# Holding back expert loads until the first gather, splitting expert 0's weights earlier, clearing row tiles earlier

## The chip, the cores and the metric

The kernel runs on one core of a Trainium2 chip. The metric is the device time of one execution in microseconds (us). The core's engines are named as the profile names them: PE (TensorE, matmul), DVE (VectorE), ACT (ScalarE), POOL (GpSimd) and SP (SyncE, which here only issues transfers). Each engine runs its own list of instructions in order. Transfers between the chip's memory and the core's are done by 16 DMA engines; an instruction on SP or POOL only starts them.

## The reference

The program is one decoder block: a forgetting attention and an S5 state-space mixer in parallel, whose result is projected by `w_out` and added to the input, and then a mixture of experts. The change touches the last product, the routing and the experts:

```
g_prob = softmax(xt @ w_rg + b_rg);  g_top, g_sel = top_k(g_prob, 1)      # 1 of 4 groups
e_prob = softmax(logits of the 8 experts of that group)
e_top, e_idx = top_k(e_prob, 2);  w = g_top * e_top / sum(e_top)
for e in range(32):
    h = silu(xt @ w_gate[e]) * (xt @ w_up[e])         # (1024, 256)
    y = y + combine[:, e:e+1] * (h @ w_down[e])       # (1024, 1024)
```

There are 1024 tokens of 1024 numbers. An expert's weights are `w_gate` and `w_up` (1024 x 256 each) and `w_down` (256 x 1024), together 3 MB in float32. All 32 experts' weights, 96 MB, are read once.

## The kernel before

The last third of the program has two stages.

**Routing.** The product with `w_out` runs in 16 units (`units`), half a row block of 128 tokens each. Behind each unit come the pieces of `tail(i)`: residual, norm, router, softmax, the choice of two experts and the place of each token in its expert's list. They leave the normed rows `xn_d` in the chip's memory (the last block's two halves are stored by SP, L1276 and L1275) and, at the very end, the table `ix`: for each expert the row numbers of up to 96 tokens (L1311, DVE).

**Experts.** For each of 32 experts POOL gathers its rows by an indirect transfer (`gather_rows`, L1328, issued two experts ahead) into one of three tiles `XG`; PE transposes them (`turn_rows`, L1339), ACT copies the transposed rows as `xh` (L1342) and DVE makes the remainder `xl` (L1343), which in all gives each operand as a high and a low part. Then `gate_up` (24 matmuls, L1352 to L1354), `hidden` (silu on ACT, product `hh` on DVE, transposition, copy `hT` on ACT, L1368), `down` (8 matmuls, L1377) and a scatter that adds the rows into the output (L1379, POOL).

**Weights.** `load_expert` issues six transfers of 512 KB for an expert on SP: four tiles `raw_e` (gate and up, each in two halves, L1083) and two tiles `wd` (down, L1087). There are five sets of these tiles, so loads run up to five experts ahead; a load waits until its tile is free, and all those behind it on SP wait with it. `split_expert` turns an expert's `raw_e` tiles into a high part `weh` by 8 casts on ACT (L1101) and a low part `wel` by 8 subtractions on DVE (L1102), 4 of each for either half; the first half is `raw_e` 0 and 1, which the first matmuls of `gate_up` use.

**What sets the order.** The program is written in Python, and a scheduler orders each engine's instructions by priorities in which program order counts; `after(...)` puts the instructions of its block behind a given one, and `keep_in_program_order` keeps the loads on SP in the order in which they are written. The table `AHEAD` says in front of which unit how many loads of which expert are written: `8: [(2, 6)]` means six of expert 2 ahead of unit 8. Expert o's remaining loads follow in the expert loop by calls `load(o, n)`.

Before, `AHEAD` puts all loads of experts 0 to 3 and four of expert 4 among the units, and expert 4's two `wd` loads behind the last unit. The tiles `XG` are cleared by POOL (`rows_tile`, L1321): two behind the routing, the third behind the second gather. Expert 0's weights are split behind `ix`, and expert 1's first half behind that.

Of the kernel before, what the change touches and what calls it, by code (L numbers as in the profile page):

```python
# [10 lines left out]
F32 = mybir.dt.float32  # L11
# [5 lines left out]
ALU = mybir.AluOpType  # L17
AX = mybir.AxisListType

P = 128  # L20
D = 1024
S = 1024
# [11 lines left out]
NE = 32  # L34
# [8 lines left out]
def hybrid_block(ctx: ExitStack, tc: tile.TileContext, t, out):  # L43

    nc = tc.nc

    def pool(stack, name, bufs=1, side=None, space=None):
        kw = {}
        if side:
            kw["side"] = side  # L50
        if space is not None:
            kw["space"] = space
        return stack.enter_context(tc.tile_pool(name=name, bufs=bufs, **kw))
# [6 lines left out]
    def mmtile():  # L60
        return psA.tile([P, 512], F32, tag="A", name="psA_t")

    def smtile():
        return psB.tile([P, 512], F32, tag="B", name="psB_t")

    def f32(ap):
        return ap.bitcast(F32)
# [4 lines left out]
    def slot(name, shape=(S,), dt=F32, where=None):  # L72
        pl, n = where or (slab, SLOTS)
        return pl.tile([P] + list(shape), dt, tag="s4", name=name, bufs=n)
# [12 lines left out]
    sp = pool(ssm_stack, "ssm_c", 1, side="right")  # L87
# [398 lines left out]
    with ExitStack() as st:  # L486
# [19 lines left out]
        for b in range(G // GB):  # L506
# [84 lines left out]
            for q4 in range(GB // 4):  # L591
# [7 lines left out]
                for r in range(4):  # L599
                    g = q4 * 4 + r  # L600
                    o = ps[:, r * P:(r + 1) * P]
# [376 lines left out]
    SR = (slabR, SLOTSR)  # L978
# [85 lines left out]
    for a in range(2):  # L1064
        nc.gpsimd.iota(ent[:, :, a, 0:1], pattern=[[P, NT], [0, 1]], base=0, channel_multiplier=1,
                       allow_small_or_imprecise_dtypes=True)
    xn_d = tc.dram_tile([S, D], F32, name="xn_d")
    tbl_d = tc.dram_tile([NE * CAP * NBLK, 2], F32, name="tbl_d")


    def load_expert(e, raws, wd):


        if isinstance(e, int):
            sel = lambda ap: ap[e]
        else:
            sel = lambda ap: ap[bass.ds(e, 1)].rearrange("o a b -> (o a) b")
        wd3 = sel(t["w_expert_down"]).rearrange("(p j) f -> p j f", j=2)
        for q in range(4):
            nm = ("w_expert_gate", "w_expert_up")[q % 2]  # L1080
            src = sel(t[nm]).rearrange("(p k) f -> p k f", k=KD)[:, q // 2 * 4:q // 2 * 4 + 4, :]
            raws[q] = raws[q]()
            tc.keep_in_program_order(nc.sync.dma_start(raws[q], src))  # L1083
            yield raws, wd
        for j in range(2):
            wd[j] = wd[j]()
            tc.keep_in_program_order(nc.sync.dma_start(wd[j], wd3[:, j, :]))  # L1087
            yield raws, wd

    def split_expert(raws, c):  # L1090

        ws = []
        for k2 in range(4):
            v = (2 * c + k2 // 2) % 3, k2 % 2
            if v not in ws_t:
                ws_t[v] = slot("weh", (2, 512), F32R), slot("wel", (2, 512), F32R)
            wh, wl = ws_t[v]
            for q in range(2):
                src = raws[k2 // 2 * 2 + q][:, k2 % 2 * 2:k2 % 2 * 2 + 2, :]
                d_ = (slice(None), slice(None), slice(q * 256, q * 256 + 256))  # L1100
                nc.scalar.copy(wh[d_], src)  # L1101
                nc.vector.tensor_tensor(wl[d_], src, f32(wh[d_]), ALU.subtract)  # L1102
            ws.append((wh, wl))
            if k2 == 1:
                yield
        yield ws
# [3 lines left out]
    def place_of(nm, shape, tiles, c, where):  # L1110
        def get():
            if c not in tiles:
# [8 lines left out]
    ahead = [load_expert(ORDER[o], [place_of("raw_e", (4, 256), raw_t, (SET[o], q), RAW[SET[o]][q]) for q in range(4)],  # L1121
                         [place_of("wd", (S,), wd_t, (o % 5, j), WD[o % 5][j]) for j in range(2)]) for o in range(NE)]
    got = []
    AHEAD = {0: [(0, 6)], 2: [(1, 6)], 8: [(2, 6)], 12: [(3, 6), (4, 2)], 14: [(4, 2)]}

    ix = rp.tile([CAP, NE], I32, name="ix")
    wts = rp.tile([CAP, NE], F32, name="wts")
    empty = rp.tile([P, NE], F32, name="empty")
    cnt = rp.tile([P, NE], F32, name="cnt")
    ptab = mmtile()  # L1130
    with ExitStack() as st:
        xp = pool(st, "x1p", 1, side="right")
# [16 lines left out]
        def product(i, n):  # L1149
            if i not in x1s:  # L1150
                x1s[i] = slot("x1", where=(SR, S2)[i - NT + 2]) if i >= NT - 2 else xp.tile([P, D], F32, name="x1", bufs=2)
                nc.gpsimd.dma_start(x1s[i], t["x"][i * P:(i + 1) * P, :])
            x1 = x1s[i]
            ns = slice(n * 512, n * 512 + 512)
            ps = mmtile()
            for k in range(KD):
                if k == KD // 2:
                    yield
                mh, ml = [v[k // 4, i // 2][:, k % 4, i % 2 * P:i % 2 * P + P] for v in (mxh, mxl)]
                wh, wl = [v[:, k % 2, :] for v in wos[n, k // 2]]  # L1160
                nc.tensor.matmul(ps, mh, wh, start=(k == 0), stop=False)
                nc.tensor.matmul(ps, mh, wl, start=False, stop=False)
                nc.tensor.matmul(ps, ml, wh, start=False, stop=(k == KD - 1))
            nc.vector.tensor_tensor(x1[:, ns], ps, x1[:, ns], ALU.add)
# [113 lines left out]
        ends = {}  # L1278
# [12 lines left out]
        for u, (i, n) in enumerate(units):  # L1291
            for o, m in AHEAD.get(u, ()):
                for _ in range(m):
                    r_ = next(ahead[o])
                got[o:] = [r_]
            pr = product(i, n)
            next(pr)
            if u == 1:
                out_splits(3)
            behind_products(u)  # L1300
            for _ in pr:
                pass
        behind_products(len(units))
        behind_products(len(units) + 1)
        for _ in range(2):
            r_ = next(ahead[4])

        pc = smtile()
        nc.tensor.matmul(pc[:, 0:NE], oneb, run, start=True, stop=True)
# [1 line left out]
        last_dve = nc.vector.tensor_tensor(ix, ptab[0:CAP, 0:NE], empty[0:CAP], ALU.add)  # L1311
# [2 lines left out]


    em_ = pool(ctx, "moe", 1, side="right")
    XG = []

    def rows_tile(where):
        XG.append(where.tile([P, S], F32, name="XG") if where is em_ else slot("XG", where=where))  # L1320
        nc.gpsimd.memset(XG[-1], 0.0)  # L1321

    rows_tile(SR)
    rows_tile(SR)
    mt = pool(ctx, "moet", 2, side="right")

    def gather_rows(xg, ix):
# [4 lines left out]
    def turn_rows(xg):  # L1332

        xh = mt.tile([P, KD, CAP], F32R, name="xh")
        xl = mt.tile([P, KD, CAP], F32R, name="xl")
        for kk in range(2):
            ps = smtile()
            for r in range(4):
                pe = nc.tensor.transpose(ps[:, r * CAP:(r + 1) * CAP], xg[0:CAP, kk * 4 + r::8], ident[0:CAP, 0:CAP])  # L1339
            dst = (slice(None), slice(kk * 4, kk * 4 + 4))  # L1340
            pv = ps[:, 0:4 * CAP].rearrange("p (a b) -> p a b", a=4)
            nc.scalar.copy(xh[dst], pv)  # L1342
            nc.vector.tensor_tensor(xl[dst], pv, f32(xh[dst]), ALU.subtract)  # L1343
        return (xh, xl), pe

    def gate_up(x, ws):
        xh, xl = x
# [40 lines left out]
    def icol(o):  # L1388
        return ix[:, ORDER[o]:ORDER[o] + 1]


    def after(*instructions):

        st = ExitStack()
        for ins in instructions:
            st.enter_context(tc.issue_after(ins.ins))
        return st

    for o in range(2):
        last_gather = gather_rows(XG[o], icol(o))  # L1400
    with tc.issue_after(last_gather.ins):
        rows_tile(em_)
    w_now = got[0]
    got.append(r_)
    got.extend([None] * (NE - 5))

    def load(o, n):
        if o < NE:
            for _ in range(n):
                got[o] = next(ahead[o])  # L1410
    with after(ends["act"], last_dve):
        *_, ws = split_expert(got[0][0], 0)
    load(5, 4)
    x, _ = turn_rows(XG[0])
    sp = split_expert(got[1][0], 1)
    next(sp)
    load(6, 2)
    behind, act, dve = None, ends["act"], last_dve
    scs = []
    for o in range(NE):  # L1420
        if o + 2 < NE:
            gather_rows(XG[(o + 2) % 3], icol(o + 2))
        ps, pe = gate_up(x, ws)
        if o + 1 < NE:
            w_next = got[o + 1]
            if o:
                with after(act, dve):
                    sp = split_expert(w_next[0], o + 1)
                    next(sp)
                load(o + 6, 2)  # L1430
        h = hidden(ps)
        dve = next(h)
        if o + 1 < NE:
            with after(pe):
                x, pe = turn_rows(XG[(o + 1) % 3])
        if behind:
            with after(pe):
                _, sc, pe = down(*behind, apart=scs[-3:])
            scs.append(sc)
            load(o + 4, 2)  # L1440
        with after(pe):
            hT, act = next(h)
        e = ORDER[o]
        behind = (hT, w_now[1], icol(o), wts[:, e:e + 1])
        if o + 1 < NE:
            with after(act, dve):
                ws = next(sp)
            load(o + 6, 2)
        w_now = w_next
# [66 lines left out]
```

## Time and profile before

| | |
|---|---|
| median of 3 runs | 1205.27 us (1204.71 to 1208.66) |
| the profiled execution | 1208.14 us, span of its instructions 1206.4 us |
| mean granted TensorE clock | 0.97 of full speed |
| PE busy | 1116.5 us, 93% of the span |
| DVE, ACT, POOL busy | 793.5, 619.5, 432.1 us |
| all transfers | 193.78 MB, of which 96 MB (in units of 1024 x 1024) are expert weights |

A share of the span is an average over many stages. In a row of the timeline, "x8" after the shapes says that eight instructions in a row were put together, the number in front of the engine is their length from first start to last end, and the bracket gives the idle time of the engine before them and what ended it. The profile's times count from the span's start; the routing ends and the expert loop begins at about 850 us.

### The profile page before, as it was taken

What the parts mean: (1) busy time and instruction counts of PE and PEld (TensorE: products, weight loads), DVE (VectorE), ACT (ScalarE), POOL (GpSimd) and SP (SyncE); (2) the same over time, 40 slices, a digit from 0 to 9 for tenths busy, and PEclk for the clock granted to TensorE, in tenths of its full rate; (3) what the DMA queues carried; (4) which work ended last, traced back from release to release, by engine and by line L of the source; (5) the groups of instructions that cost most, each with busy time, mean ns of one, the idle gap of its engine ahead of it and who ended that gap; (6) DMA issues with size and microseconds to landing.
All of it is one profiled execution on the core that took longest, in us unless ns stands there. A gap on an engine that the chain in (4) does not pass through costs nothing. (4 is left out here: it accounts for less than half of the span.)

```text
span 1206.4 us, 15940 instructions
## 1 busy us (share of the span) xinstructions
PE 1116.5 (93%) x5323; PEld 854.3 (71%) x5324; DVE 793.5 (66%) x1561; ACT 619.5 (51%) x1195; POOL 432.1 (36%) x431
## 2 busy tenths in 40 slices
PE   5899899899999999999899988998499999999995
PEld 4678778687898778888677777886366666666562
DVE  4657577667025889898987696538566666666661
ACT  5423332332335576766769553103366666666662
POOL 3025445432514474656714362103322222222211
PEclk9899899999999999999989999999699999999998
DMA  8516435330253012000622539564599999999992
GB/s 234 82 41 157 92 75 104 80 91 28 87 121 53 2 27 47 11 23 28 210 70 101 175 124 346 189 220 179 185 306 341 333 312 317 312 310 320 310 332 51
DMA packets 100919, 193.78 MB, mean 161 GB/s; under 512 B 26177, under 2 KB 55169, under 8 KB 100833
## 3 DMA queue, kind: packets, MB, share of 16 engines
q1 hardware_dynamic: 82176, 150.16, 40.8%
q0 software_dynamic: 14048, 34.17, 10.5%
q10 hardware_dynamic: 4608, 8.39, 1.9%
q8 instruction: 43, 0.70, 0.2%
q14 instruction: 44, 0.35, 0.1%
HBM read 164.30 MB, written 35.52 MB: 166 GB/s over the span
## 5 line engine op out<-in xcount | busy, mean ns | idle before, releaser
L1102 DVE TENSOR_TENSOR wel<-raw_e,weh 128x512 fp32r<-128x512 f32 x256 | 157.4, 684 | 118.8 <-ACT weh L1101 107.5
L1101 ACT CAST weh<-raw_e 128x512 fp32r<-128x512 f32 x256 | 137.0, 621 | 3.0 <-DMA raw_e<-in_w_expert_up 1.8
L910 POOL TENSOR_TENSOR sm<-sm,pe 128x256 f32<-128x256 f32 (+2 forms) x80 | 96.4, 1205 | 72.5 <-ACT pe L907 64.2
L1377 PE MATMUL psA_t<-wd,hT 128*96 128x512 f32 x256 | 117.4, 600 | 3.1 <-DMA wd<-in_w_expert_down 2.3
L1352 PE MATMUL psA_t<-weh,xh 128*96 128x512 f32 x256 | 103.7, 405 | 0.2
L1353 PE MATMUL psA_t<-wel,xh 128*96 128x512 f32 x256 | 102.0, 399 | 0.0
L183 PE MATMUL psA_t<-hTh,wgl 128*128 128x512 f32 x256 | 101.9, 398 | 0.0
L182 PE MATMUL psA_t<-hTh,wgh 128*128 128x512 f32 x256 | 101.4, 396 | 0.0
L1354 PE MATMUL psA_t<-weh,xl 128*96 128x512 f32 x256 | 101.2, 395 | 0.0
L184 PE MATMUL psA_t<-hTl,wgh 128*128 128x512 f32 x256 | 100.8, 394 | 0.0
L1379 POOL DMA_INDIRECT out_rows<-R,ix x32 | 46.1, 1441 | 128.5 <-ACT hT L1368 117.2
L793 PE MATMUL psA_t<-wqh,hTh 128*128 128x384 f32 x256 | 88.3, 345 | 0.0
L794 PE MATMUL psA_t<-wql,hTh 128*128 128x384 f32 x256 | 86.8, 339 | 0.0
L795 PE MATMUL psA_t<-wqh,hTl 128*128 128x384 f32 x256 | 86.8, 339 | 0.0
L1328 POOL DMA_INDIRECT XG<-xn_d,ix x32 | 36.5, 1140 | 139.7 <-PE psB_t L1339 132.3
L1378 ACT ACTIVATE R<-psA_t,wts 96x512 f32<-96x512 f32 x64 | 43.7, 682 | 77.1 <-PE psA_t L1377 75.0
L1377 PEld LDWEIGHTS psA_t<-wd,hT 128*96 128x96 f32 x256 | 40.4, 168 | 56.4 <-issue 49.0
L905 ACT ACTIVATE pH<-psB_t 128x512 fp32r<-128x512 f32 (+1 forms) x96 | 49.1, 512 | 38.9 <-PE psB_t L902 38.7
L908 DVE TENSOR_TENSOR pL<-pe,pH 128x256 fp32r<-128x256 f32 (+2 forms) x80 | 62.9, 798 | 6.8 <-ACT pe L907 5.9
L855 DVE TENSOR_REDUCE mx<-psB_t 128x1 f32<-128x512 f32 (+2 forms) x96 | 51.2, 550 | 7.9 <-PE psB_t L850 4.2
L183 PEld LDWEIGHTS psA_t<-hTh,wgl 128*128 128x128 f32 x256 | 48.7, 190 | 9.5 <-POOL wgl L172 0.2
L184 PEld LDWEIGHTS psA_t<-hTl,wgh 128*128 128x128 f32 x256 | 48.5, 189 | 9.5
(427 smaller groups left out, 2878.2 us busy)
## 6 DMA issues: line engine op xcount, KB each, us to landing
raw_e<-in_w_expert_gate SPq DMA_DIRECT2D x64, 512.0 KB
raw_e<-in_w_expert_up SPq DMA_DIRECT2D x64, 512.0 KB
wd<-in_w_expert_down SPq DMA_DIRECT2D x64, 512.0 KB
gate_d<-ge ACTq DMA_DIRECT2D x32, 256.0 KB
gt<-gate_d SPq DMA_DIRECT2D x16, 512.0 KB
raw_g<-in_w_in SPq DMA_DIRECT2D x12, 512.0 KB
raw_q<-in_w_in SPq DMA_DIRECT2D x48, 128.0 KB
x<-in_x SPq DMA_DIRECT2D x8, 512.0 KB
```

The costliest lines, as they stand in the source:

```text
L182: nc.tensor.matmul(ps, wh, hTh[k][:, ns], start=(k == 0), stop=False)
L183: nc.tensor.matmul(ps, wl, hTh[k][:, ns], start=False, stop=False)
L184: nc.tensor.matmul(ps, wh, hTl[k][:, ns], start=False, stop=(k == KD - 1))
L793: nc.tensor.matmul(ps[:, :384], ah, wh, start=(k == 0), stop=False)
L794: nc.tensor.matmul(ps[:, :384], ah, wl, start=False, stop=False)
L910: nc.gpsimd.tensor_tensor(sm[:, o0:], sm[:, o0:], pe[:, :n], ALU.add)
L1101: nc.scalar.copy(wh[d_], src)
L1102: nc.vector.tensor_tensor(wl[d_], src, f32(wh[d_]), ALU.subtract)
L1352: nc.tensor.matmul(ps, xh[:, k, :], wh[:, k % 2, :], start=(k == 0), stop=False)
L1353: nc.tensor.matmul(ps, xh[:, k, :], wl[:, k % 2, :], start=False, stop=False)
L1354: last = nc.tensor.matmul(ps, xl[:, k, :], wh[:, k % 2, :], start=False, stop=(k == KD - 1))
L1377: pe = nc.tensor.matmul(po, hT[:, j, :], wd[j][:, ns], start=(j == 0), stop=(j == 1))
```

## The change

1. `AHEAD` keeps only the loads of experts 0 and 1 and the four `raw_e` of expert 2. The 14 others of experts 2 to 4 (two `wd` of expert 2, six each of experts 3 and 4) are written behind the first two gathers and behind a new small transfer `first_d` on SP, which reads a few numbers of `XG[0]` and so cannot start before the first gather has landed.
2. `XG[0]` and `XG[1]` are cleared ahead of unit 8.
3. Expert 0's `split_expert` is written ahead of unit 12 (before: behind `ix`).
4. Expert 1's first half is split behind the last `xl` of the first `turn_rows`.

```diff
@@ module level
+    first_d = tc.dram_tile([1, 8], F32, name="first_d")
...
-    AHEAD = {0: [(0, 6)], 2: [(1, 6)], 8: [(2, 6)], 12: [(3, 6), (4, 2)], 14: [(4, 2)]}
+    AHEAD = {0: [(0, 6)], 2: [(1, 6)], 8: [(2, 4)]}
...
@@ loop over units
+            if u == 8:
+                rows_tile(SR)
+                rows_tile(SR)
+            if u == 12:
+                *_, ws = split_expert(got[0][0], 0)
             pr = product(i, n)
...
@@ behind the units
-        for _ in range(2):
-            r_ = next(ahead[4])
...
-    rows_tile(SR)
-    rows_tile(SR)
...
@@ turn_rows
-            nc.vector.tensor_tensor(xl[dst], pv, f32(xh[dst]), ALU.subtract)
-        return (xh, xl), pe
+            dve = nc.vector.tensor_tensor(xl[dst], pv, f32(xh[dst]), ALU.subtract)
+        return (xh, xl), pe, dve
...
@@ behind the first two gathers
-    with after(ends["act"], last_dve):
-        *_, ws = split_expert(got[0][0], 0)
+
+    tc.keep_in_program_order(nc.sync.dma_start(first_d, XG[0][0:1, 0:8]))
+    load(2, 2)
+    load(3, 6)
+    load(4, 6)
     load(5, 4)
-    x, _ = turn_rows(XG[0])
-    sp = split_expert(got[1][0], 1)
-    next(sp)
+    x, _, dve = turn_rows(XG[0])
+    with after(dve):
+        sp = split_expert(got[1][0], 1)
+        next(sp)
     load(6, 2)
```

How this moves instructions shows at two places. On SP, around the stores of the last normed rows (`xn_d`), before: `raw_e_7612` to `wd_7622` are expert 3's loads, `raw_e_7624` to `raw_e_7752` expert 4's.

```order
L1083 DMA raw_e_7612<-in_w_expert_gate 128x1024
L1083 DMA raw_e_7614<-in_w_expert_up 128x1024
L1083 DMA raw_e_7616<-in_w_expert_gate 128x1024
L1083 DMA raw_e_7618<-in_w_expert_up 128x1024
L1087 DMA wd_7620<-in_w_expert_down 128x1024
L1087 DMA wd_7622<-in_w_expert_down 128x1024
L1083 DMA raw_e_7624<-in_w_expert_gate 128x1024
L1083 DMA raw_e_7626<-in_w_expert_up 128x1024
L1083 DMA raw_e_7750<-in_w_expert_gate 128x1024
L1083 DMA raw_e_7752<-in_w_expert_up 128x1024
L1276 DMA xn_d_6787<-xn1_8067 128x512
L1275 DMA xn_d_6787<-xn1_8067 128x512
```

The same place after the change, where `wd_8100` and `wd_8102` are expert 2's, and `raw_e_8104` to `raw_e_8110` expert 3's:

```order
L1283 DMA xn_d_6787<-xn1_8072 128x512
L1282 DMA xn_d_6787<-xn1_8072 128x512
L1466 TENSOR_LOAD cnti_10868
L1466 ISA x2
L1413 DMA first_d_6788<-XG_7366 1x8
L1088 DMA wd_8100<-in_w_expert_down 128x1024
L1088 DMA wd_8102<-in_w_expert_down 128x1024
L1084 DMA raw_e_8104<-in_w_expert_gate 128x1024
L1084 DMA raw_e_8106<-in_w_expert_up 128x1024
L1084 DMA raw_e_8108<-in_w_expert_gate 128x1024
L1084 DMA raw_e_8110<-in_w_expert_up 128x1024
L1088 DMA wd_8112<-in_w_expert_down 128x1024
```

The stores come without loads ahead of them; the loads of experts 3 and 4, and expert 2's `wd`, stand behind `first_d`, and expert 5's and all later ones behind those.

On ACT, where expert 0's first product begins, before: `raw_e_6906` and `6908` are expert 1's first half, `raw_e_6910` its second; the first two `xh` are expert 0's rows, the next two expert 1's, and `hT2` is expert 0's.

```order
L1101 CAST weh_8146<-raw_e_6906 128x2x256
L1101 CAST weh_8146<-raw_e_6908 128x2x256
L1342 CAST xh_8130<-psB_t_8132 128x384
L1101 CAST weh_8152<-raw_e_6906 128x2x256
L1342 CAST xh_8130<-psB_t_8139 128x384
L1101 CAST weh_8152<-raw_e_6908 128x2x256
L1360 ACT_TABLE_LOAD
L1360 ACTIVATE si_8188<-psA_t_8163 96x256
L1342 CAST xh_8192<-psB_t_8194 128x384
L1342 CAST xh_8192<-psB_t_8201 128x384
L1368 COPY hT2_8211<-psB_t_8208 128x192
L1101 CAST weh_8102<-raw_e_6910 128x2x256
```

The same place after the change, from expert 0's `hT2` on: here `raw_e_6907` and `6909` are expert 1's first half, `6911` and `6913` its second, `7358` and `7360` expert 2's first half.

```order
L1370 COPY hT2_8213<-psB_t_8210 128x192
L1102 CAST weh_7613<-raw_e_6911 128x2x256
L1102 CAST weh_7613<-raw_e_6913 128x2x256
L1102 CAST weh_7619<-raw_e_6911 128x2x256
L1102 CAST weh_7619<-raw_e_6913 128x2x256
L1102 CAST weh_7625<-raw_e_7358 128x2x256
L1102 CAST weh_7625<-raw_e_7360 128x2x256
L1102 CAST weh_7631<-raw_e_7358 128x2x256
L1102 CAST weh_7631<-raw_e_7360 128x2x256
L1102 CAST weh_8148<-raw_e_6907 128x2x256
L1102 CAST weh_8148<-raw_e_6909 128x2x256
L1102 CAST weh_8154<-raw_e_6907 128x2x256
```

Expert 1's first half is cast behind expert 0's `hT2`, and behind eight casts of its own second half and of expert 2's first half; before, it was cast ahead of expert 0's silu. DVE's subtractions stand in the same order as the casts.

## Rows read from the trace of the kernel before

**Rows 1.** Windows: busy us (instructions) by engine, granted clock, DMA share, GB/s
```profile
...
800.00:810.00 10.00, 10.00 (x51) 8.25 (x50) 2.00 (x4) 0.37 (x1) 0.00 (x0) 1.00 0.62 205
850.00:860.00 10.00, 0.00 (x0) 0.00 (x0) 5.14 (x9) 1.44 (x3) 8.54 (x4) 0.50 0.71 246
860.00:870.00 10.00, 7.98 (x27) 5.56 (x28) 3.37 (x10) 3.18 (x5) 0.96 (x1) 0.60 0.56 160
870.00:880.00 10.00, 9.88 (x51) 7.27 (x50) 7.42 (x14) 7.08 (x15) 1.47 (x2) 1.00 0.47 141
...
```

**Rows 2.** Timeline, end of the routing (start, length, engine, line, ..., idle before <- releaser)
```profile
...
840.72 3.03 DVE L1258 TENSOR_SCALAR te<-oh,ent 128x32 f32<-128x32 f32 x1
841.87 1.83 POOL L1321 MEMSET XG<- 128x1024 f32 x2
...
849.44 0.19 DVE L1311 TENSOR_TENSOR ix<-psA_t,empty 96x32 int32<-96x32 f32 x1 [0.60 <-PE psA_t L1263]
...
849.64 5.49 DVE L1102 TENSOR_TENSOR wel<-raw_e,weh 128x512 fp32r<-128x512 f32 x9
850.51 5.60 POOL L1328 DMA_INDIRECT XG<-xn_d,ix  x1 [6.81 <-DVE wel L1102]
...
861.97 1.52 PE L1339 MATMUL psB_t<-ident,XG 96*128 96x96 f32 x8 [12.57 <-DMA XG<-xn_d,ix]
...
863.54 0.74 PE L1352 MATMUL psA_t<-weh,xh 128*96 128x512 f32 x1
...
```

**Rows 3.** The gather's line: durations in ns, and times from issue to landing
```profile
...
L1328 POOL DMA_INDIRECT XG<-xn_d,ix x32: 956/977/5604, 850.5 to 1141.8; - x32
...
DMA to landing us min/median/max: 4.0/5.4/11.3
```

**Rows 4.** Timeline, experts 0 and 1
```profile
...
871.40 0.38 ACT L1360 ACTIVATE si<-psA_t 96x256 f32<-96x256 f32 x1 [5.20 <-PE psA_t L1354]
...
873.27 4.27 ACT L1101 CAST weh<-raw_e 128x512 fp32r<-128x512 f32 x8
...
873.93 4.91 DVE L1102 TENSOR_TENSOR wel<-raw_e,weh 128x512 fp32r<-128x512 f32 x8 [0.58 <-ACT weh L1101]
...
878.19 1.02 PE L1339 MATMUL psB_t<-ident,XG 96*128 96x96 f32 x8
...
```

**Rows 5.** Windows: a burst, the gap, the expert loop's long stretches
```profile
...
730.00:740.00 10.00, 7.58 (x41) 6.28 (x42) 5.96 (x10) 5.01 (x9) 0.47 (x1) 1.00 0.99 370
853.00:860.00 7.00, 0.00 (x0) 0.00 (x0) 2.14 (x4) 0.00 (x0) 6.04 (x4) 0.50 0.93 323
880.00:922.00 42.00, 42.00 (x174) 25.88 (x173) 25.38 (x45) 28.82 (x57) 10.18 (x9) 1.00 1.01 334
943.00:1125.00 182.00, 182.00 (x763) 114.03 (x762) 112.69 (x198) 127.33 (x254) 43.56 (x36) 1.00 0.99 316
...
```

**Rows 6.** SyncE's timeline: issues of an expert's two wd loads
```profile
...
881.82 1.19 SPq L1087 DMA_DIRECT2D wd<-in_w_expert_down  x2
...
891.88 1.19 SPq L1087 DMA_DIRECT2D wd<-in_w_expert_down  x2
...
943.49 1.62 SPq L1087 DMA_DIRECT2D wd<-in_w_expert_down  x2
...
1125.53 3.79 SPq L1087 DMA_DIRECT2D wd<-in_w_expert_down  x2
```

**Rows 7.** PE's timeline: its longest wait for a load in the expert loop
```profile
...
1144.62 4.39 PE L1377 MATMUL psA_t<-wd,hT 128*96 128x512 f32 x6 [1.44 <-DMA wd<-in_w_expert_down]
...
```

**Rows 8.** Windows of 2 us at the end of the loads
```profile
...
1174.00:1176.00 2.00, 2.00 (x14) 1.55 (x13) 2.00 (x5) 1.27 (x4) 0.00 (x0) 1.00 0.81 250
1178.00:1180.00 2.00, 2.00 (x9) 1.18 (x8) 0.00 (x0) 0.97 (x4) 0.00 (x0) 1.00 0.32 131
...
```

**Rows 9.** Timeline, the last expert
```profile
...
1179.95 2.18 ACT L1101 CAST weh<-raw_e 128x512 fp32r<-128x512 f32 x4
...
1189.31 3.67 PE L1377 MATMUL psA_t<-wd,hT 128*96 128x512 f32 x8 [0.78 <-ACT hT L1368]
...
```

More of the change, by code (lines that the diff above doesn't have):

```diff
@@ L1129, in hybrid_block, with rows_tile @@
     cnt = rp.tile([P, NE], F32, name="cnt")
+    XG = []
+    def rows_tile(where):
+        XG.append(slot("XG", where=where) if where is SR else where.tile([P, S], F32, name="XG"))
+        nc.gpsimd.memset(XG[-1], 0.0)
     ptab = mmtile()
@@ L1316, in hybrid_block @@
     em_ = pool(ctx, "moe", 1, side="right")
[L1317 to L1321, printed above, removed]
-    rows_tile(SR)
-    rows_tile(SR)
     mt = pool(ctx, "moet", 2, side="right")
@@ L1403, in hybrid_block @@
     w_now = got[0]
-    got.append(r_)
-    got.extend([None] * (NE - 5))
+    got.extend([None] * (NE - 3))
     def load(o, n):
@@ L1434, in hybrid_block @@
             with after(pe):
-                x, pe = turn_rows(XG[(o + 1) % 3])
+                x, pe, _ = turn_rows(XG[(o + 1) % 3])
         if behind:
```

## The prediction

> **What bounds the kernel now.** The page gives PE 93% of the span, which says nothing about the stage that changes, so I read the windows of 10 us first. From 850 to 860 us PE does nothing, and its granted clock is 0.50, the lower level of 1.2 GHz; in the next 10 us it is 0.60, then 1.00 again [rows 1]. The timeline of that stretch names the wait: PE's first transposition starts at 861.97 after 12.57 us of idleness, released by the landing of the first gather [rows 2]. That gather had been issued at 850.51, 1.07 us after `ix`, kept POOL for 5.60 us where the line's median is 0.98, and landed 11.3 us after its issue where the shortest takes 4.0 [rows 2, 3].
>
> The long windows show the second limit. From 880 to 1125 us PE is busy throughout, but so are the DMA engines: share 1.01 and then 0.99, at 334 and 316 GB/s [rows 5]. SP's issues tell which of the two falls behind. An expert's `wd` loads come 10.06 us apart early (881.82 to 891.88), which is PE's pace; from 943.49 to 1125.53 fifteen experts take 182.04 us, 12.14 each [rows 6], while PE stays at its pace. So the lead of the loads shrinks by 2.08 us for each expert, and at 1144.62 PE does wait 1.44 us for `wd` [rows 7]. Before the loop the engines are not full: 0.62 in 800 to 810, and after the gap 0.56 and 0.47 [rows 1]. The loads that are issued ahead of 850 are the lead on which the loop then lives.
>
> The end: the loads' traffic falls from 0.81 to 0.32 between 1175 and 1179 [rows 8]; the last expert's second half is cast at 1179.95, and its `down` starts at 1189.31 [rows 9].
>
> **The change part by part.**
>
> *Clearing earlier.* The two clearings take 1.83 us on POOL at 841.87, and a small operation of DVE beside them takes 3.03 us and ends at 843.75, just behind them, so they stand in the way of the routing's last tail [rows 2]. With them gone everything up to `ix` comes 1.8 us earlier: 847.6 instead of 849.44. Where they go POOL is nearly idle (0.00 us busy from 800 to 810) [rows 1]; I take nothing for that.
>
> *Expert 0's split earlier.* Eight casts of 4.27 us and eight subtractions of 4.91 us [rows 4] move to a stretch where ACT is busy 0.37 and DVE 2.00 of 10 us, while PE is full [rows 1]. That hides them; without that cover they would cost 5 us once. What they leave behind is a DVE with nothing to do when the gather is issued. In the trace the subtractions run from 849.64 to 855.13 and the gather ends at 856.11, which is 855.13 plus the usual 0.98 [rows 2, 3]: it looks held by them. So I let the gather start at 847.6 + 1.07 = 848.7 and take 0.98, and since no load is in the queues, land after the shortest time of 4.0: 852.7. PE's first transposition then starts 9.2 us earlier, at 852.8.
>
> There is a reading against that: the 5.60 us may be the price of the first gather of the program, whatever runs beside it, for only one of 32 was long [rows 3]. Then PE starts at 857.4. The Trainium skill has a rule that would give this: in "GPSIMD Engine Reference", section "Instruction dispatch", the first call of freshly loaded code on that engine pays about 6 us more. The trace neither shows nor excludes a loading of code here; this is rival 2.
>
> *Expert 1's first half later.* Here the gain goes again. Before, expert 1's first half was cast ahead of expert 0's silu, and PE went from one expert's product straight into the next. Afterwards the four casts that PE needs stand on ACT behind expert 0's `hT` and eight other casts (the order above). From the transposition to the silu behind the product took 871.40 - 861.97 = 9.4 us in before, on a low clock at first [rows 1, 2, 4]; so 862.2. From silu to the first cast behind `hT` took 1.87 us [rows 4]: casts from 864.1. Eight take 4.27, two more 1.1, and DVE's subtractions run at 4.91 / 8 = 0.61 each from 0.66 behind [rows 4]: the first matmul pair has its high part at 869.5 and its low part at 870.9. PE has stood still for about 7 us by then, so I give the product the 7.9 us that the first one took from 863.54 to the silu [rows 2, 4]: 878.6, its first matmul aside. Before, it ended at 878.19 [rows 4]. The 9.2 us are eaten up: 0. At the full clock the second product of before took at most 878.19 - 871.40 = 6.8 us [rows 1, 4], which would make it -1.
>
> *The held loads.* Fourteen loads of 0.524 MB, 7.34 MB, that ran in 800 to 850 now start when the first gather has landed, at about 853. The fastest 10 us in the rows move 370 GB/s [rows 5], so they need 19.8 us (at the loop's 334 it would be 22.0). From 853 to 880 there are 27 us; the traffic of before fills 0.93 x 7 + 5.6 + 4.7 = 16.8 of them [rows 1, 5], which leaves 10.2. So at 880 the queue is 19.8 - 10.2 = 9.6 us behind that of before. SP's wait for the landing and the first load's way cost about 1 more by my estimate, between nothing and the 4.0 of a gather [rows 3]: 10.6. Behind `first_d` stand on SP the fourteen loads and then expert 5's; the earliest of them that is needed is expert 2's `wd`, by the third `down`, 2 x 10.06 us behind the first one, which follows the transposition at 878.19 [rows 4, 6], so near 899, and all fourteen have landed by 875: no engine waits for them directly. Can the loop give it back? From 880 to 922 the engines move 334 GB/s on PE's demand; if they could do 370 they would win back 42 x (1 - 334/370) = 4.1, if they are full as the share of 1.01 says, nothing; I take 2. That leaves 8.6.
>
> A later queue costs nothing until the lead is used up; with 2.08 us per expert that is now 8.6 / 2.08, some four experts earlier. From there PE moves at the loads' 12.14 us, and the end follows the loads. What the end of before had in hand must be taken off. The loads end at about 1179 [rows 8]; the four `wd` behind the last `raw_e` are 4 x 1.42 = 5.7 us of traffic, so the last `raw_e` lands between 1173 and 1177, 3 to 7 us ahead of its cast at 1179.95 [rows 9]. I take 3.5, since transfers in flight share the engines and end together. That makes 5.1. When PE waits its clock falls: at 1144.62 six matmuls took 4.39 us after a wait of 1.44 [rows 7] where eight take 3.67 [rows 9], so 1.6 more. In a stretch where loads bind, only the last such wait counts: +1.6.
>
> **The sum:** PE at the first `down` 0, loads +5.1, clock +1.6: about +7. On the profiled execution's 1208.14 that is 1215; that execution lies 2.9 above the median of 1205.27, and on the median the forecast is 1212.
>
> **Rivals.**
>
> 1. *Faster: the loads are not the bound.* If the engines take the fourteen loads faster than any row here shows, or win back 4 us in 880 to 922 and 3 more later, the lag is below what the end has in hand, and only PE counts. With expert 1's casts arriving as worked out it is 0 to -1; only if gate and up of expert 1 hardly wait does the start's 9.2 us stay, and 1196 follows. Against it: a share near 1.0 for 300 us [rows 5]. It decides where the lag at 925 is under 3 us. Chance 0.13, over 1196 to 1201.
>
> 2. *The first gather stays long.* Then PE and the held loads both start 4.6 us later, which nothing in the sum absorbs: 1212 + 4.6 = 1217. For it: one long gather, the first. Against it: the end at 855.13 + 0.98. Chance 0.25.
>
> 3. *No change.* The lag at the end equals what there was in hand (7 us instead of 3.5, or 4 won back instead of 2), and PE is even: 1204 to 1208. Chance 0.2. It would look the same if `first_d` held nothing back; the order shows that it does.
>
> The forecast itself, 1209 to 1215, has 0.42.
>
> **The numbers.** Within 0.3%, about what a measurement of this kernel can tell from no change, is 1201.7 to 1208.9. Slower by more has the forecast and rival 2: 0.67; the same 0.2; faster 0.13. Low end: the upper part of rival 1, 1201, leaves 0.11 out. High end: the loads at the loop's 334 GB/s add 2.2, nothing won back adds 2 and a long gather 4.6 to 1212, together 1221; 0.07 lie above.
>
> **What would show it.** Right: `ix` about 1.8 us earlier; a first gather of 0.98 us, and PE's transposition near 853; a wait of PE for the casts (`weh`) of some 7 us ahead of expert 1's product; a DMA share near 1.0 from 854 on; the first wait of PE for `wd` or of ACT for `raw_e` several experts earlier than 1144; last `wd` issues 6 to 10 us later. Wrong: no wait of PE for casts behind expert 0 (then that step failed); a share well below 1.0 between 870 and 900 (then the backlog was smaller than worked out, and rivals 1 or 3 follow); a first gather still near 5.6.

## The result and the profile after

The changed kernel took 1214.38 us (median of 13 runs, 1205.84 to 1218.15), the kernel before 1205.39 us (13 runs, 1199.90 to 1208.66): ratio 1.0072, 95% interval 1.0052 to 1.0093, or 8.7 us more (6.3 to 11.2). The profiled execution took 1214.09 us with a span of 1212.3, 5.95 more than that of before, at the same mean clock (0.969 against 0.970). The pair of profiles shows less than the medians because of where the two executions lie: the profiled one of before is 2.75 us above the median of its runs, that of after 0.29 below.

The timeline where the expert loop begins, after; it answers to [rows 2, 4]:

```profile
...
840.65 1.24 DVE L1265 TENSOR_SCALAR te<-oh,ent 128x32 f32<-128x32 f32 x1
...
847.63 0.19 DVE L1321 TENSOR_TENSOR ix<-psA_t,empty 96x32 int32<-96x32 f32 x1 [0.60 <-PE psA_t L1270]
...
848.12 1.10 POOL L1330 DMA_INDIRECT XG<-xn_d,ix  x1 [6.27 <-DVE nblk L1459]
...
852.57 0.27 SPq L1413 DMA_DIRECT2D first_d<-XG  x1
...
852.69 1.51 PE L1341 MATMUL psB_t<-ident,XG 96*128 96x96 f32 x8 [5.09 <-DMA XG<-xn_d,ix]
852.95 0.82 SPq L1088 DMA_DIRECT2D wd<-in_w_expert_down  x2
...
861.36 0.38 ACT L1362 ACTIVATE si<-psA_t 96x256 f32<-96x256 f32 x1 [5.34 <-PE psA_t L1356]
...
862.98 6.34 ACT L1102 CAST weh<-raw_e 128x512 fp32r<-128x512 f32 x12
863.63 7.32 DVE L1103 TENSOR_TENSOR wel<-raw_e,weh 128x512 fp32r<-128x512 f32 x12 [0.33 <-ACT weh L1102]
...
868.33 0.74 PE L1354 MATMUL psA_t<-weh,xh 128*96 128x512 f32 x1 [5.60 <-ACT weh L1102]
...
869.80 0.74 PE L1355 MATMUL psA_t<-wel,xh 128*96 128x512 f32 x1 [0.73 <-DVE wel L1103]
...
877.19 1.02 PE L1341 MATMUL psB_t<-ident,XG 96*128 96x96 f32 x8
...
878.05 2.31 PE L1379 MATMUL psA_t<-wd,hT 128*96 128x512 f32 x5
...
```

`ix` comes 1.8 us earlier, the gather keeps POOL for 1.10 us instead of 5.60, and PE's first transposition starts at 852.69 instead of 861.97 [rows 2]. Then PE stands for 5.60 us, because expert 1's high part `weh` is cast behind `hT`, and for 0.73 more for `wel`. Expert 1's product ends at 877.19, where PE goes on to the next rows; before, that was 878.19 [rows 4]. So a start that came 9.3 us earlier is worth 1.0 us two products later.

Windows after, with the columns of [rows 1]:

```profile
...
800.00:810.00 10.00, 10.00 (x51) 8.11 (x50) 6.51 (x12) 4.83 (x9) 0.00 (x0) 1.00 0.00 0
850.00:860.00 10.00, 7.26 (x27) 5.15 (x28) 1.08 (x2) 2.24 (x3) 3.41 (x4) 0.65 0.78 251
860.00:870.00 10.00, 3.60 (x18) 2.44 (x17) 7.81 (x14) 7.85 (x16) 0.96 (x1) 0.86 1.02 326
870.00:880.00 10.00, 10.00 (x36) 6.50 (x37) 2.39 (x5) 1.33 (x4) 0.96 (x1) 0.79 1.03 409
853.00:880.00 27.00, 20.56 (x79) 13.75 (x78) 11.28 (x20) 11.43 (x23) 2.87 (x3) 0.80 0.99 349
880.00:922.00 42.00, 42.00 (x175) 26.05 (x174) 25.04 (x44) 28.87 (x58) 9.74 (x8) 1.00 1.02 348
943.00:1125.00 182.00, 177.96 (x729) 110.44 (x728) 109.21 (x192) 122.64 (x245) 42.65 (x35) 0.98 0.99 315
...
1174.00:1176.00 2.00, 2.00 (x9) 1.08 (x8) 0.00 (x0) 0.97 (x3) 0.00 (x0) 1.00 1.03 393
...
1184.00:1186.00 2.00, 2.00 (x9) 1.07 (x8) 0.00 (x0) 0.97 (x3) 0.00 (x0) 1.00 0.44 180
...
```

The stretch from 853 to 880 in before:

```profile
...
853.00:880.00 27.00, 17.85 (x77) 12.83 (x78) 12.93 (x28) 10.26 (x20) 8.48 (x7) 0.72 0.62 195
...
```

From 800 to 810, where expert 0's split now stands beside a full PE, nothing is loaded any more: 0 GB/s against 205 [rows 1]. From 853 to 880 the DMA share is 0.99 at 349 GB/s, where before it was 0.62 at 195, and 409 GB/s are reached from 870 to 880. In the long stretch PE has lost 4.04 of 182 us [rows 5]. The traffic runs on at 1.03 at 1175, where it was 0.81 before, and falls only at 1185 [rows 8].

SyncE's issues of `wd`, each the counterpart of one in [rows 6], and the last four of the program, after and then before:

```profile
...
882.29 2.31 SPq L1088 DMA_DIRECT2D wd<-in_w_expert_down  x2
...
893.63 2.96 SPq L1088 DMA_DIRECT2D wd<-in_w_expert_down  x2
...
952.32 1.87 SPq L1088 DMA_DIRECT2D wd<-in_w_expert_down  x2
...
1135.03 1.78 SPq L1088 DMA_DIRECT2D wd<-in_w_expert_down  x2
...
1173.56 4.51 SPq L1088 DMA_DIRECT2D wd<-in_w_expert_down  x4
```

```profile
...
1165.08 6.10 SPq L1087 DMA_DIRECT2D wd<-in_w_expert_down  x4
...
```

The first four are 0.5, 1.8, 8.8 and 9.5 us late [rows 6]: the lag builds up between 882 and 943 and then stays. The last four come at 1173.56 instead of 1165.08, 8.5 late.

PE's waits from 845 us on (total us, times, longest):

```profile
...
PE psA_t L1379 <- DMA wd<-in_w_expert_down: 6.2, 4, 2.1
PE psA_t L1354 <- ACT weh L1102: 5.6, 1, 5.6
...
```

Its three long waits for `wd` (a fourth, at 1137.93, is 0.41 us), the last casts of the program, and a window with the columns of [rows 1]:

```profile
...
1072.37 4.36 PE L1379 MATMUL psA_t<-wd,hT 128*96 128x512 f32 x6 [2.05 <-DMA wd<-in_w_expert_down]
...
1106.35 4.43 PE L1379 MATMUL psA_t<-wd,hT 128*96 128x512 f32 x6 [1.99 <-DMA wd<-in_w_expert_down]
...
1140.78 4.28 PE L1379 MATMUL psA_t<-wd,hT 128*96 128x512 f32 x6 [1.75 <-DMA wd<-in_w_expert_down]
...
1186.13 2.18 ACT L1102 CAST weh<-raw_e 128x512 fp32r<-128x512 f32 x4
...
```

```profile
...
1072.37:1076.73 4.36, 4.36 (x9) 1.77 (x9) 0.00 (x0) 0.68 (x1) 0.00 (x0) 0.64 0.99 304
...
```

Before, PE waits for `wd` at 1132.12 (0.38 us), 1142.09 (0.52) and 1144.62 (1.44, [rows 7]), 2.3 us in all. Counted in PE's transpositions, of which each expert has one group, the first wait comes behind the 22nd instead of the 28th: six experts earlier. Between these stops PE keeps its own pace of 10.07 us per expert. The experts with a stop take 13.90, 13.89 and 14.15 us (from 1068.44, 1102.47 and 1136.50), before 10.68 and 14.06 (from 1129.86 and 1140.54). So a stop of some 2 us costs nearly 4: behind it six matmuls take 4.36 us at a mean granted clock of 0.64, where eight take 3.67 at the end of before [rows 9]. After loses 11.7 us in this way and before 4.6; the 7.1 more, less the 1.0 gained at the start, are what the last casts moved, from 1179.95 [rows 9] to 1186.13. Behind the last stop PE waits for no load in either kernel.

### The profile page after: what moved, and what is told of

It is laid out like the page before. It is cut to its first block, busy times and chain, and to the rows that moved or that the text cites. A ratio compares the mean times of both kernels' runs of the same rounds, so it can differ in the third digit from the quotient of the medians.

```text
span 1212.3 us, 15936 instructions
## 1 busy us (share of the span) xinstructions
PE 1121.8 (93%) x5323; PEld 856.9 (71%) x5324; DVE 791.3 (65%) x1561; ACT 619.9 (51%) x1195; POOL 428.4 (35%) x431
## 5 line engine op out<-in xcount | busy, mean ns | idle before, releaser
L1379 PE MATMUL psA_t<-wd,hT 128*96 128x512 f32 x256 | 120.7, 614 | 7.0 <-DMA wd<-in_w_expert_down 6.2
L1330 POOL DMA_INDIRECT XG<-xn_d,ix x32 | 31.9, 998 | 145.0 <-PE psB_t L1341 134.9
L1354 PEld LDWEIGHTS psA_t<-weh,xh 128*96 128x96 f32 x256 | 43.2, 169 | 22.5 <-ACT weh L1102 5.8
L1168 PE MATMUL psA_t<-woh,mxh 128*128 128x512 f32 x128 | 54.3, 424 | 1.2 <-DVE gt L986 1.2
```

The source lines that it names most:

```text
L1354: nc.tensor.matmul(ps, xh[:, k, :], wh[:, k % 2, :], start=(k == 0), stop=False)
L1379: pe = nc.tensor.matmul(po, hT[:, j, :], wd[j][:, ns], start=(j == 0), stop=(j == 1))
```

## The experiments

The theory (**loads**): the time is set by when the loads get through the DMA engines; holding 14 of them makes the whole queue late, and PE's earlier start can't help. Rivals: **start** (PE's start decides, and the change fails only because expert 1's casts come late), and **no bound** (the time went to something else that the change moved). Each was timed beside the kernel before, and the ratio compares with those runs. Columns: the table `ix`, PE's first transposition, the first `down`, the last issue of `wd`, the span (all of the profiled execution, us), and the ratio to before.

| kernel | ix | PE | down | last wd | span | ratio (95%) |
|---|---|---|---|---|---|---|
| before | 849.4 | 862.0 | 879.1 | 1165.1 | 1206.4 | 1 |
| after | 847.6 | 852.7 | 878.1 | 1173.6 | 1212.3 | 1.0072 (1.0052 to 1.0093) |
| a_loads_early | 855.3 | 859.9 | 876.0 | 1165.5 | 1205.1 | 0.9967 (0.9947 to 0.9986) |
| c_hold_cast1_early | 848.3 | 853.0 | 869.2 | 1173.4 | 1216.2 | 1.0067 (1.0046 to 1.0089) |
| d_early_cast1_early | 855.2 | 865.5 | 882.8 | 1171.1 | 1209.7 | 1.0038 (1.0017 to 1.0059) |
| e_hold_six | 852.2 | 858.7 | 874.8 | 1170.6 | 1212.1 | 1.0033 (1.0015 to 1.0052) |
| f_before_hold_only | 851.0 | 860.5 | 885.5 | 1178.9 | 1220.3 | 1.0181 (1.0149 to 1.0213) |
| g_before_fewer_bytes | 851.5 | 864.2 | 880.4 | 1134.3 | 1202.6 | 0.9948 (0.9928 to 0.9967) |
| h_after_fewer_bytes | 849.0 | 853.8 | 879.1 | 1135.3 | 1202.1 | 0.9942 (0.9916 to 0.9968) |
| i_loads_early_clean | 861.8 | 868.7 | 884.7 | 1172.8 | 1214.1 | 1.0042 (1.0020 to 1.0064) |
| j_more_lead | 856.9 | 862.9 | 879.4 | 1164.7 | 1206.3 | 1.0006 (0.9980 to 1.0033) |
| k_early_clear_later | 845.1 | 856.5 | 873.5 | 1160.6 | 1201.9 | 0.9997 (0.9977 to 1.0017) |
| l_more_lead_clear_later | 845.9 | 857.8 | 874.3 | 1159.5 | 1200.8 | 1.0000 (0.9979 to 1.0022) |
| m_hold_six_tail | 846.5 | 853.1 | 870.1 | 1158.8 | 1196.9 | 0.9944 (0.9921 to 0.9967) |

Two rows show what the time goes with: c and m are at the first `down` within 1 us of each other, but their last `wd` go out 14.6 us apart, and their ratios are 1.0067 and 0.9944. The ratios stand on 6 to 13 runs of each kernel, the other columns on one execution.

**The hold taken out of after** (a_loads_early).

```diff
-    AHEAD = {0: [(0, 6)], 2: [(1, 6)], 8: [(2, 4)]}
+    AHEAD = {0: [(0, 6)], 2: [(1, 6)], 8: [(2, 6)], 12: [(3, 6), (4, 2)], 14: [(4, 2)]}
...
-    tc.keep_in_program_order(nc.sync.dma_start(first_d, XG[0][0:1, 0:8]))
-    load(2, 2)
-    load(3, 6)
-    load(4, 6)
```

> The changed kernel with the loads where they were before (nothing held, no first_d); the two other moves stay. The loads theory (the end follows the loads' queue in the expert loop): the first gather issues near 848 and takes about 1 us; since loads are in flight it lands after 5 to 8 us, so PE starts near 854; expert 1's first half is cast early again, so PE does not wait before expert 1's product and stands 5 to 8 us ahead of before at the first down. The loads are no later than before, and those that wait for free tiles come earlier with PE, so the end comes 3 to 8 us earlier than before: 1197 to 1202. The start theory (the time is lost where PE waits for expert 1's casts, and holding the loads costs nothing by itself) expects the same 5 to 8 us, 1197 to 1200. Should it come out near the changed kernel's 1214, both are wrong and the early split or the early clearing costs the time.

1204.36 us against 1206.79: 0.33% faster than before, some 4 us and so at the low end of the 3 to 8 expected, and 1.0% faster than after by the ratios. The last `wd` go out where those of before do. The size is muddied: `ix` came 7.7 us later than in after.

**Hold kept, expert 1's first half cast early** (c_hold_cast1_early; d_early_cast1_early is the same edit on a).

```diff
             if u == 12:
                 *_, ws = split_expert(got[0][0], 0)
+            if u == 14:
+                sp = split_expert(got[1][0], 1)
+                next(sp)
...
-    with after(dve):
-        sp = split_expert(got[1][0], 1)
-        next(sp)
```

> The changed kernel, loads held as there, but expert 1's first half is split ahead of unit 14, so its casts are done before the first gather lands. The loads theory: PE loses its wait of 5.6 us before expert 1's product and is at the first down near 871 instead of 878, but the loads are as late as in the changed kernel, so PE meets them some three experts earlier and the end moves by less than 3 us: 1211 to 1214. The start theory: the 7 us come back, 1206 to 1208. This run tells the two apart.

PE's wait for `weh` is gone and the first `down` is 9 us earlier, yet the ratio is after's. SP's last issue and PE's waits for `wd` in c:

```profile
...
1173.39 5.93 SPq L1088 DMA_DIRECT2D wd<-in_w_expert_down  x4
```

```profile
...
PE psA_t L1382 <- DMA wd<-in_w_expert_down: 14.5, 10, 2.0
...
```

The last issue is after's within 0.2 us, and PE waits 14.5 us for `wd` instead of 6.2: the 8.3 more are nearly the 9 that it came earlier. This refutes the start theory for after.

> Loads as before, clearing and expert 0's split as in the changed kernel, and expert 1's first half split ahead of unit 14. The loads theory: like the first of these runs or 1 us better, since the raw tiles of expert 1 come free earlier and two of expert 6's loads can start before 850: 1195 to 1201. The start theory: no different from that run.

Expected was a gain, measured a loss of 0.38%. `ix` came 5.7 us later than in before, PE 3.5 and the last `wd` 6.0. Loads run at most five experts ahead, and tiles come free only as PE goes on, so a late start would delay loads too; that fits, but no run tests it alone.

**Only expert 4's six held** (e_hold_six).

```diff
+    AHEAD = {0: [(0, 6)], 2: [(1, 6)], 8: [(2, 6)], 12: [(3, 6)]}
...
     tc.keep_in_program_order(nc.sync.dma_start(first_d, XG[0][0:1, 0:8]))
-    load(2, 2)
-    load(3, 6)
     load(4, 6)
```

> The changed kernel with only expert 4's six loads held; the eight of experts 2 and 3 start early as before. Six loads are 6 x 1.42 = 8.5 us of traffic, and the stretch from 853 to 880 had 10.2 us free. The loads theory: no lag against before at 880, so the end is that of before or a little earlier, 1200 to 1206, and not in proportion (six of fourteen of 9 us would be 4 us slower than before, 1209). The start theory: it depends on where expert 1's casts stand; here they stand ahead of expert 0's silu, so 5 to 8 us faster than before, 1197 to 1200.

Slower than expected, by 4 us against before. The first gather landed at 858.7, not near 853, so the held loads started 6 us later than I had reckoned, and the last `wd` were 5.5 late. The lag lies between those of before and after, as the loads theory wants. But 4 us is also what six fourteenths of the whole hold would cost, which the expectation had ruled out. `ix` came 4.5 us later than in after, and this run does not part the two.

**The hold alone, in before** (f_before_hold_only): `AHEAD` and the lines behind the gathers as in after, nothing else changed.

```diff
+    AHEAD = {0: [(0, 6)], 2: [(1, 6)], 8: [(2, 4)]}
...
+    tc.keep_in_program_order(nc.sync.dma_start(first_d, XG[0][0:1, 0:8]))
+    load(2, 2)
+    load(3, 6)
+    load(4, 6)
     load(5, 4)
```

> The kernel before with the hold alone: the fourteen loads behind first_d, expert 0's split and the clearing where they were. The first gather lands later than in the changed kernel (row table 1.8 us later, and 4.6 us more while DVE subtracts): PE starts near 859 and the loads at 859. The loads theory: 6 us more lag than in the changed kernel, so 1218 to 1222. The start theory: PE gets through experts 0 and 1 some 6 us later than in the changed kernel, the same number; but a loss much smaller than in the changed kernel would say that the hold is not what costs. It also shows whether the hold alone puts expert 1's first casts behind expert 0's hT.

It took 1.81% more than before, 1227 us by the ratio, where 1218 to 1222 were expected. The profiled span grew by 13.9 us and the timed median by 20, because the profiled execution of f is the fastest of its six runs, 3.6 us below their median (1225.60), and that of before is above its own. The last `wd` go out 5.3 us behind those of after, near the 6 expected; why the time grew by more stays open. Its timeline:

```profile
...
851.20 4.89 DVE L1103 TENSOR_TENSOR wel<-raw_e,weh 128x512 fp32r<-128x512 f32 x8
851.47 5.59 POOL L1327 DMA_INDIRECT XG<-xn_d,ix  x1 [6.26 <-DVE wts L1311]
...
875.91 0.74 PE L1351 MATMUL psA_t<-weh,xh 128*96 128x512 f32 x1 [5.60 <-ACT weh L1102]
...
```

The gather is long again, beside the subtractions, and ends 0.97 us behind the last of them. And PE waits 5.60 us for `weh` though expert 1's split was not touched; in a, which keeps the change's `after(dve)` without the hold, PE has no such wait. So it is the hold that puts expert 1's casts behind `hT`; holding only six loads (e, m) does not, as PE has no such wait there.

**A sixth fewer bytes in the loop** (g_before_fewer_bytes; h_after_fewer_bytes is the same in after).

```diff
-            tc.keep_in_program_order(nc.sync.dma_start(wd[j], wd3[:, j, :]))
+            if j == 0 or not isinstance(e, int) or e not in ORDER[5:]:
+                tc.keep_in_program_order(nc.sync.dma_start(wd[j], wd3[:, j, :]))
```

> The kernel before, with the second wd load left out for the experts from the sixth on (27 of 192 loads, 14 MB; the product uses what an earlier expert left there). With five loads for an expert instead of six, the loads need 10.1 us of traffic where PE needs 10.06, so they no longer fall behind. The loads theory: the waits of the end of the loop and the low clock behind them go, some 4 us: 1200 to 1203. The start theory: the same. It is the base for the next run.

> The changed kernel with the same loads left out. The loads theory: the lag of the held loads no longer reaches the end, so only PE's place at the first down counts, which is 1.0 us earlier than before (878.05 against 879.05): 1 us faster than the run above, within 2 of it, and 10 to 13 us faster than the changed kernel. The start theory (PE's wait for expert 1's casts costs the time): it stays 8 to 9 us slower than the run above.

The change costs nothing then: 1201.7 and 1201.9 us. Windows of g and of h:

```profile
...
943.00:1100.00 157.00, 157.00 (x657) 98.56 (x656) 97.33 (x171) 110.93 (x221) 37.75 (x31) 1.00 0.98 317
1120.00:1160.00 40.00, 40.00 (x169) 25.09 (x168) 24.84 (x45) 28.01 (x57) 8.69 (x7) 1.00 0.60 168
...
```

```profile
...
943.00:1100.00 157.00, 157.00 (x661) 98.98 (x660) 98.36 (x173) 110.71 (x221) 37.75 (x31) 1.00 0.98 310
1120.00:1160.00 40.00, 40.00 (x168) 25.00 (x167) 24.77 (x44) 28.15 (x56) 8.69 (x7) 1.00 0.70 209
...
```

PE is full in both, waits for no `wd` from its first transposition to the end, and later on the DMA share falls to 0.60 and 0.70. In h it still stands 5.60 us for `weh`, as in after. This is the cleanest test: the 0.72% exist only where loads bind, and the "no bound" theory is out.

**Towards a better version** (i_loads_early_clean, j_more_lead). i is a with expert 0's split written ahead of unit 12's loads; j also issues expert 5's four `raw_e` ahead of unit 14.

```diff
         for u, (i, n) in enumerate(units):
+            if u == 12:
+                *_, ws = split_expert(got[0][0], 0)
             for o, m in AHEAD.get(u, ()):
...
-            if u == 12:
-                *_, ws = split_expert(got[0][0], 0)
```

> The changed kernel without the hold, as the first run of the study, but with expert 0's split written ahead of the loads of unit 12, so that it keeps its place between the units and does not stand in the last tails, where it made the row table 6 us late. The loads theory: row table at 847 to 849, PE's first transposition at 853 to 857 (other loads are in flight), first down at 870 to 874, and loads no later than before: 1196 to 1201, below the first run's 1203. If it is not faster than that run, the place of expert 0's split did not matter.

> The run above with expert 5's four raw loads written ahead of unit 14: their tiles are free once expert 0 is split. They use 5.7 us of the engines' idle time ahead of 850. The loads theory: the loads' end moves up by up to 5 us; PE's own pace from the first down gives a floor of some 1193 to 1196. So 1193 to 1198, 2 to 5 us below the run above. If loads were not the bound, no difference from it.

Both missed by 10 us and more: 1213.93 and 1208.25 us. In i `ix` came at 861.8. POOL's timeline in i:

```profile
...
814.84 0.53 POOL L1207 DMA_DIRECT2D out_rows<-x  x1 [23.69 <-DVE x L1171]
...
816.66 0.96 POOL L1135 MEMSET XG<- 128x1024 f32 x1 [0.20 <-PE psA_t L1170]
...
819.67 0.55 POOL L1159 DMA_DIRECT2D x<-in_x  x1 [1.02 <-PE psA_t L1170]
...
```

POOL stands 23.69 us for DVE ahead of a store; the second clearing comes behind that store, waits 0.20 for PE itself, and the load of `x` for the last rows stands behind both (819.67; in after it went out at 788.34, ahead of the same store, and the store at 816.26). j is 4.3 us faster than i, about the step expected for more lead, but its `ix` came 4.9 earlier too, so the two can't be told apart.

**The clearings later** (k_early_clear_later is i, l_more_lead_clear_later is j, with this edit).

```diff
-            if u == 8:
+            if u == 12:
                 rows_tile(SR)
+            if u == 13:
                 rows_tile(SR)
```

> No hold, expert 0's split ahead of the loads of unit 12, and the row tiles cleared from units 12 and 13 on instead of unit 8, behind POOL's last loads of x. In the two earlier runs without the hold the second clearing waited on POOL until 816 for its memory, with the load of x for the last rows behind it, and the row table came 8 to 14 us late. The loads theory: row table back at 847 to 851, first down at 870 to 875, loads as early as before: 1197 to 1203. If the row table is still late, something else holds the routing up, and the time is near 1208 to 1214.

> The run above with expert 5's four raw loads ahead of unit 14. The loads theory: 3 to 6 us below the run above, down to PE's own pace: 1193 to 1199.

`ix` came back to 845 and 846, so the clearings had been the cause. The gain did not follow: both ratios are 1.00. Their profiled spans are 4.5 and 5.6 us shorter than before's, but most of that is the choice of executions: the profiled ones lie 1.0 and 2.7 us below their medians, that of before 2.75 above. Part of what an early `ix` could give is lost at the first gather, in k:

```profile
...
847.78 1.10 POOL L1333 DMA_INDIRECT XG<-xn_d,ix  x1 [6.78 <-DVE cnti L1465]
...
856.53 1.52 PE L1344 MATMUL psB_t<-ident,XG 96*128 96x96 f32 x8 [11.52 <-DMA XG<-xn_d,ix]
...
```

```profile
...
846.00:848.00 2.00, 0.00 (x0) 0.00 (x0) 0.63 (x5) 0.00 (x0) 0.22 (x1) 0.50 1.02 418
848.00:850.00 2.00, 0.00 (x0) 0.00 (x0) 0.00 (x0) 0.00 (x0) 1.70 (x2) 0.50 1.03 420
850.00:852.00 2.00, 0.00 (x0) 0.00 (x0) 0.00 (x0) 0.00 (x0) 1.73 (x3) 0.50 1.03 416
...
```

The loads issued from 842 to 846 fill the engines (share 1.02 and 1.03, up to 420 GB/s), and the gather needs 8.75 us from issue to PE instead of after's 4.57. In l it takes 4.47, but goes out only at 853.28, 7.4 us behind `ix`: DVE, ahead of it, waits 6.32 us, by the profile for an `xn_d` store to land.

**Six loads held, those that k has in flight there** (m_hold_six_tail): expert 4's `wd` and expert 5's `raw_e`, on k.

```diff
-        for _ in range(2):
-            r_ = next(ahead[4])
...
+    tc.keep_in_program_order(nc.sync.dma_start(first_d, XG[0][0:1, 0:8]))
+    load(4, 2)
     load(5, 4)
```

> The run with the early split and the later clearing, but the six loads that stood there between 842 and 846 (expert 4's wd, expert 5's raw) wait behind first_d; the other twelve run early. They need 6 x 1.42 = 8.5 us, and in that run the engines had some 9.7 us idle between 850 and 880. The loads theory: no lag to speak of at 880. The first gather, with nothing in flight, lands 4 to 5 us after its issue instead of 8.7, PE starts near 852.5 instead of 856.5 and is at the first down near 869. As the loads bind at the end the gain is small: 1199 to 1205, at most 4 us below that run and not slower than it. If it is 4 us or more slower, even six held loads cost what the fourteen did in proportion, and the idle time between 850 and 880 cannot be used.

1199.32 us against 1206.53: 0.56% faster than before (0.33 to 0.79), 1.3% faster than after by the ratios. The gather in m, and the engines meanwhile:

```profile
...
848.84 1.10 POOL L1331 DMA_INDIRECT XG<-xn_d,ix  x1 [6.42 <-DVE cnti L1464]
...
852.96 0.27 SPq L1414 DMA_DIRECT2D first_d<-XG  x1
...
853.08 1.52 PE L1342 MATMUL psB_t<-ident,XG 96*128 96x96 f32 x8 [6.66 <-DMA XG<-xn_d,ix]
...
```

```profile
...
848.00:850.00 2.00, 0.00 (x0) 0.00 (x0) 0.63 (x5) 0.00 (x0) 1.10 (x1) 0.50 0.00 0
850.00:852.00 2.00, 0.00 (x0) 0.00 (x0) 0.00 (x0) 0.00 (x0) 1.76 (x2) 0.50 0.37 103
...
```

With the engines empty when it is issued, the gather takes 4.24 us. The last `wd` go out at 1158.8, 6.3 earlier than in before: 12 of the 14 loads run in the routing again, PE starts 8.9 us earlier and does not wait for casts. Against k, which lacks only this hold, PE starts 3.4 us earlier and the ratio is 0.53% lower.

## Why the prediction was right

The forecast was 1212 us (+7 on the median), measured 1214.4 (+9.0; the profiled pair +5.95). The mechanism held: the loads bind, the start's gain is eaten up, the lag reaches the end. How the lag reaches PE was otherwise than worked out, and errors of a few us offset each other, so part of the closeness is luck. Step by step:

- **Clearing earlier:** -1.8 us at `ix`, measured 1.81, and at the place that was read: `te` takes 1.24 us instead of 3.03. That it costs nothing where it goes held for after; in i `ix` was 16.7 us later than in k, which moves only the clearings.
- **First gather:** 0.98 us, landing at 852.7; measured 1.10 and PE at 852.69. That it agrees to 0.1 us is luck: the gather went out 0.49 us behind `ix`, not 1.07, and PE started 4.57 behind its issue, not 4.0. Rival 2 (first use) is refuted: the gather took 5.59 to 5.60 us in the three kernels (before, f, g) where DVE's subtractions ran beside it, and 1.10 in the eleven others, each time as the first of the program.
- **Expert 1's casts late:** a wait of about 7, measured 5.60 and 0.73; product end 878.6, measured 877.2. The sum's 0 was -1. But c shows that this step decided nothing: without the wait the time is the same. The order was read rightly; that the hold causes it, and not the diff's `after(dve)`, only f and a showed.
- **Held loads:** a lag of 8.6 in the loop, measured 8.8 at 943, 9.5 at 1125 and 8.5 at the last issue. The way there was nearly as worked out: from 853 to 880 the engines moved 349 GB/s, less than the 370 taken, and 154 more than before. That is 4.2 of the 7.34 MB; the other 3.2 are 9 us at 349, where the sum had 9.6.
- **From the lag to the end:** the sum lets PE move at the loads' 12.14 us from the first wait on. The trace has PE at 10.07 with three stops, so the end follows from the number and the price of the stops. The 3.5 in hand at the end appears in the trace only as what is left, 8.5 less the 6.2 that the last casts moved, that is 2.3; no wait for a load stands near the end. That transfers in flight end together, the reason for taking 3.5, no run shows.
- **Clock:** +1.6 for one wait, the last, which before has too (1144.62). Measured, each of the three stops pays it: of the 7.1 us that PE loses beyond before, 3.9 are idle time and the other 3.3 slower work behind the stops. PE's mean granted clock from 943 to 1125 was 0.98 against 1.00. Loads and clock together were 6.7 in the sum, and 7.1 measured, less the 1.0 at the start.
- **First wait for `wd`:** some four experts earlier than 1144.62, measured seven, or six from first wait to first wait.
- **Rivals 1 and 3** needed a lag under 3 us at 925, or one that the end had in hand; it was 8.8 at 943, and PE's last casts came 6.2 us late.

The bound itself was tested: g and h show that the loads are what the change costs, c that PE's start is not. The timed difference, 8.7, is more than the 5.95 of the profiled pair; single executions of these two kernels spread over 9 and 12 us, so a pair doesn't settle 3 us, and the sums above are those of the pair.

## What to carry to other kernels

Where a stream of loads is slower than the engine it feeds (12.14 against 10.06 us per expert), the loads issued ahead are the capital: here a hold that took 8 to 9 us from it cost more than a start 9 us earlier gave, and c shows that the start alone buys nothing then. A wait for a load also costs more than the wait: PE lost 3.8 to 4.1 us at each stop of about 2, with a granted clock of 0.64 behind the first. A latency on the path may still be worth clearing the queues for, but then hold only the few loads that would be in flight just there, as m did. Look at what stands behind an early allocation: in i a clearing of 1 us had a load behind it that came 31 us later than in after. And before two profiles are compared, see where either execution lies among its timed runs.

## What the hardware showed that was not expected

The DMA engines moved 416 to 420 GB/s with 512 KB loads and the first gather in flight (k, 846 to 852), while in the expert loop, among gathers and scatters, a share of 0.99 goes with 315. The price of a queue for a small indirect transfer: 4.24 us from its issue to PE's start with empty engines (m), 8.75 beside loads that keep them full (k). In a, where the last loads were running out, it was 4.15.

The Trainium skill, "SBUF — State Buffer", section "Who interferes with whom", says that a VectorE instruction with two SBUF inputs contends with a GpSimd instruction that reads SBUF. The long gathers agree in kind (5.60 against 1.10 us, their ends 0.97 to 0.98 behind the last subtraction). Later gathers beside such subtractions took 1.25 and 1.33 us in before (at 1131 and 1141), so what sets the size is open. The Trainium skill, "GPSIMD Engine Reference", section "Instruction dispatch", gives about 6 us for a first call of loaded code; no run here shows that for the gather.
